# A written order for TensorE, ScalarE and VectorE in the expert stage of a two-layer decoder trunk

## The chip, the core and the metric

The kernel runs on one core of a Trainium2 chip. Its time is the device time of one execution in microseconds; lower is better. The core has separate instruction queues for TensorE (PE in the profile; its weight loads have a row of their own, PEld), VectorE (DVE), ScalarE (ACT), GpSimd (POOL) and SyncE (SP, which here only starts transfers). Each queue is worked off in the order in which its instructions stand, and an instruction whose input isn't ready holds everything behind it on the same queue.

## The reference, cut to what matters

The trunk has two layers. Each has a mixer (convolution heads beside attention heads) and a channel mixer; in layer 0 that is a dense SwiGLU, in layer 1 a mixture of eight experts of which every token takes two. There are 256 tokens of width 1024, and an expert is 3584 wide, all in float32:

```
def _swiglu(h, w_gate, w_up, w_down):
    return (jax.nn.silu(h @ w_gate) * (h @ w_up)) @ w_down

for e in range(N_EXPERTS):
    out = out + gates[:, e:e + 1] * _swiglu(t, w_gate[e], w_up[e], w_down[e])
```

The experts' weights are 8 x 3 x 3584 x 1024 float32 numbers, 352 MB, and each is read once.

## The kernel before, in words

Everything up to the routing (mixer, dense layer, mixer, router) takes the first 457 us and isn't touched. After it stands the **expert stage**, a straight-line program written by `expert_steps`.

**Tiles of weights.** A weight tile is about 0.9 MB: two 128-row pieces of `w_gate` or `w_up` (128x1792 numbers) or of `w_down` (128x2048, or 128x1024 for the last piece). SyncE loads it into one of seven `raw` buffers (L73). Then it is *converted* (`Gran.conv`): ScalarE writes a rounded copy `wh` (L192), VectorE writes the rest, `wl = raw - wh` (L193). TensorE multiplies with both. There are four `wh` and four `wl` buffers, so that a fifth tile's conversion waits until TensorE is done with the first.

**Products.** `products` (L883) issues the matmuls of a tile. An expert with more than 64 tokens takes three matmuls for each piece (wh, wl, and wh with the rest of the activations); one with at most 64 takes two, with the two parts of its tokens side by side in 128 columns, and later adds the lower half of the sums to the upper. The count is known only at run time, so `by_count` (L869) puts both versions into a branch on TensorE.

**Chunks.** An expert is cut into four chunks of 896 columns. A chunk has four gate tiles, four up tiles, and the four down tiles of the same chunk of the expert before it: twelve tiles in all. Their sums stand in PSUM banks `pg`, `pu` and `pd`, two each; two banks `pt` serve everything else.

**Late work.** When a sum is complete, other work follows on it:
- `low` (L967, ScalarE) copies the lower halves of a gate or up sum out of PSUM into `lo`, and `fold_` (L973, TensorE) adds them to the upper halves;
- `post` makes SiLU of the gate sum (L982, ScalarE) and multiplies with the up sum (L984, VectorE);
- `transposes` (L934, TensorE) turns that product, and `split` copies it out in two parts (L232 ScalarE, L233 VectorE), ready for the down tiles;
- `gather` picks the next expert's tokens; `rows_of` and `scatter` split a finished expert's rows, bring them back to token order and add them to `x` (L1040, VectorE).

**What sets the order.** `add` collects steps; a step with a tile has its `Gran`, whose conversion `drive` writes at most three tiles ahead, and `add_later` puts late work behind the next tile or the one after it. The order on each engine's queue isn't this list, though: a scheduler takes these steps in their order as priorities and moves instructions between the branches by its own estimate of when they are ready:

```
            while nxt < len(grans) and nxt < done + hl[1] and grans[nxt][1] not in held:
                grans[nxt][1].conv()
                nxt += 1
```

Of the kernel before, what the change touches and what calls it, by code (L numbers as in the profile page):

```python
# [14 lines left out]
P = 128  # L15
# [31 lines left out]
def trunk_kernel(ctx: ExitStack, tc, x_in, attn_norm, ffn_norm, w_in, b_in, conv_w, conv_b,  # L47
# [811 lines left out]
    def expert_steps(rnd):  # L859

        xg, ST, gt, gg, rxs = {}, {}, {}, {}, {}

# [20 lines left out]
        def gather(e):  # L885
            def run():
                m1, pt = moe["m1"], moe["pt"]
                Sm = m1.tile([P, NT, P], F32R, name="Sm")
                slots = slot1[:, rnd, :]
                if rnd == 0:  # L890

                    slots = m1.tile([P, P], F32, name="sl")
# [4 lines left out]
                x2 = xg[e] = m1.tile([P, KD, 2, P], F32R, name="xg", bufs=2)  # L897
                for q in range(2):
                    ps = pt.tile([P, 4, P], F32, name="pt")
                    for j in range(4):  # L900
                        d = slice((4 * q + j) * P, (4 * q + j + 1) * P)
                        for t in range(NT):
                            nc.tensor.matmul(ps[:, j, :], moe["hn"][:, t, d], f32(Sm[:, t, :]), start=(t == 0),
                                             stop=(t == NT - 1))
                    xq = x2[:, 4 * q:4 * q + 4]
                    split(xq[:, :, 0, :], xq[:, :, 1, :], ps)
                if e == 0 and rnd == 0:
                    moe["flags"]()
                    moe["weights"]()
                ps = pt.tile([P, 512], F32, name="pt")  # L910

                def rms(few):
                    for rows, cols in ((slice(P), slice(P)),) + ((slice(HP), slice(0, P, 2)),) * few:
                        for t in range(NT):
                            nc.tensor.matmul(ps[rows, 0:1], f32(Sm[:, t, cols]), moe["rs"][:, t:t + 1],
                                             start=(t == 0), stop=(t == NT - 1))
                by_count(e, rms)
                rxs[e] = m1.tile([P, 1], F32, name="rx", bufs=3)
                nc.scalar.copy(rxs[e], ps[:, :1])
                ps = pt.tile([P, NT, P], F32, name="pt")  # L920
                for t in range(NT):
                    nc.tensor.transpose(ps[:, t, :], f32(Sm[:, t, :]), ident)
                ST[e] = m1.tile([P, NT, P], F32R, name="ST", bufs=3)
                nc.scalar.activation(ST[e], ps, AF.Copy)
            return run

        def transposes(e, c):
            def run():
                g = gg[e, c]
                g2 = gt[e, c] = moe["m1"].tile([P, KJ, P, 2], F32R, name="g2", bufs=NCH)  # L930
                for j0, j1 in ((0, 4), (4, KJ)):
                    ps = moe["pt"].tile([P, 4, P], F32, name="pt")
                    for j in range(j0, j1):
                        nc.tensor.transpose(ps[:, j - j0, :], g[:, j * P:(j + 1) * P], ident)  # L934
                    split(g2[:, j0:j1, :, 0], g2[:, j0:j1, :, 1], ps[:, :j1 - j0, :])
            return run

        def proj(e, c, nm, w, pool):
# [4 lines left out]
            def step(k2):  # L943
# [14 lines left out]
                add(run, Gran((rnd, e, c, nm, k2), (2, CH), lambda t: [(t, wv[:, k2 * 2:k2 * 2 + 2, :])],  # L958
                              lambda t: t, DVE))
# [8 lines left out]

            def post():
                def fold_(few):  # L970
                    if few:
                        for hc in range(2):
                            nc.tensor.matmul(st["p"][hc][:HP, :HC], fold, moe["lo"][:, hc * HC:(hc + 1) * HC],  # L973
                                             start=False, stop=True)
                if rnd == 0:
                    by_count(e, fold_)
# [11 lines left out]
        yd = {}  # L988

        def down(e, c):  # L990
            wv = moe_w_down[0, e, c * CH:(c + 1) * CH, :].rearrange("(j p) c -> p j c", p=P)
            order = [(0, (0, 1)), (2, (0, 1)), (4, (0, 1)), (6, (0, 1))]
            if (e, c) == (NE - 1, NCH - 1):

                order[2:] = [(4, (0,)), (6, (0,)), (4, (1,)), (6, (1,))]

            def step(j0, chs):
                j1 = min(j0 + 2, KJ)

                def run(wh, wl):  # L1000
# [4 lines left out]
                    def mms(few):  # L1005
                        for j in range(j0, j1):
                            g_ = gt[e, c][:, j]
                            both = g_.rearrange("p s h -> p (s h)")[:, :P]
                            for i, ch in enumerate(chs):
                                o = slice(i * 512, (i + 1) * 512)  # L1010
                                products(yd[e, ch], (g_[:, :, 0], g_[:, :, 1], both), wh[:, j - j0, o], wl[:, j - j0, o],
                                         c == 0 and j == 0, c == NCH - 1 and j == KJ - 1, few)
                    by_count(e, mms)
                add(run, Gran((rnd, e, c, "d", j0), (j1 - j0, D), lambda t: [(t, wv[:, j0:j1, :])],
                              lambda t: t[:, :, chs[0] * 512:(chs[-1] + 1) * 512], DVE))
                if (e, c, chs) == (NE - 1, NCH - 1, (0,)) and j1 == KJ:
                    add_later(1, rows_of(e, (0,)))
                    add_later(2, scatter(e, (0,)))
            return [lambda a=a: step(*a) for a in order]

        ys = {}

        def rows_of(e, halves=(0, 1)):

            def run():
                for ch in halves:
                    y = ys[e, ch] = tmp.tile([P, 2, 512], F32R, name="h", bufs=3)
                    split(y[:, 0, :], y[:, 1, :], yd[e, ch])
            return run

        def scatter(e, halves=(0, 1)):
            def run():
                for ch in halves:
                    y = ys[e, ch]
                    for t in range(NT):
                        ps = moe["pt"].tile([P, 512], F32, name="pt")
                        for i in range(2):
                            nc.tensor.matmul(ps, ST[e][:, t, :], y[:, i, :], start=(i == 0), stop=(i == 1))  # L1038
                        xs = x[:, t, ch * 512:(ch + 1) * 512]
                        nc.vector.scalar_tensor_tensor(xs, ps, moe["gates"][:, t, e:e + 1], xs,  # L1040
                                                       op0=ALU.mult, op1=ALU.add)
            return run
# [3 lines left out]
        def do(fs, n=None):  # L1046
            for _ in range(len(fs) if n is None else min(n, len(fs))):
                fs.pop(0)()

        seq = [(e, c) for e in range(NE) for c in range(NCH)]  # L1050
        add(gather(0))
        for i, (e, c) in enumerate(seq):
            g = proj(e, c, "g", moe_w_gate, "pg")
            u = proj(e, c, "u", moe_w_up, "pu")
            d = down(e - 1, c) if e > 0 else []
# [8 lines left out]
            do(d, 1)  # L1064
            do(u, 1)
            if e > 1 and c == 0:
                add(scatter(e - 2))
            if c == 2 and e + 1 < NE:
                add(gather(e + 1))
            do(u, 1)  # L1070
            do(d, 1)
            do(u, 2)
            do(d)
        for c in range(NCH):
            d = down(NE - 1, c)
            if c == 0:
                add(rows_of(NE - 2))
            do(d, 3)
            if c == 0:
                add(transposes(*seq[-1]))  # L1080
                add(scatter(NE - 2))
            do(d)
        add(rows_of(NE - 1, (1,)))
        add(scatter(NE - 1, (1,)))
# [6 lines left out]
    n0 = len(steps)  # L1091
    expert_steps(0)
    held += [g for g, _ in steps[n0:] if g is not None][:AHEAD_E + 1]
    drive()

# [15 lines left out]
    with tc.If(big > P):  # L1111
        raw_t.clear()
        expert_steps(1)
        drive()
# [28 lines left out]
```

## Time and profile before

| | us |
|---|---|
| median of 3 runs | 1554.54 (1549.16 to 1554.97) |
| the profiled execution, its own time | 1559.1 |
| its span, first to last instruction | 1557.3 |
| outside the span | 1.8 |
| expert stage from the first product on | 457 to 1557.3 |

The profiled execution is 0.3% above the median. In the profile, the share of busy time of an engine is an average over stages; the expert stage is read by itself. Idle time "before" an instruction is put down to the engine whose result came last. A matmul's duration overlaps the next one's, so its start-to-start distance says what it costs in a row of them.

### The profile page before, as it was taken

How to read it: one execution, taken by the hardware profiler on the slowest of the kernel's cores; microseconds unless marked ns; L12 is line 12 of the kernel's file. 1: busy time of each engine (PE TensorE's matmuls, PEld its weight loads, DVE VectorE, ACT ScalarE, POOL GpSimd, SP SyncE). 2: the span in 40 equal slices, each digit the busy share in tenths (PEclk: the TensorE clock that was granted, in tenths of full speed). 3: DMA queues.
4: the chain of work that ended last, by engine and by line, in shares of the span. 5: the costliest groups of instructions: out<-in, count | busy, mean ns of one | idle time of the engine just before them, and what ended most of it. 6: DMA issues, size and time to landing. Idle time of an engine off the chain costs nothing. (4 is left out here: it accounts for less than half of the span.)

```text
span 1557.3 us, 19153 instructions
## 1 busy us (share of the span) xinstructions
PE 1381.4 (89%) x6963; PEld 1135.5 (73%) x6963; DVE 1172.4 (75%) x1155; ACT 1016.8 (65%) x1120; POOL 143.4 (9%) x99
## 2 busy tenths in 40 slices
PE   7989999989969888888889988998888889888986
PEld 6768999987656666677777876776777667676765
DVE  7776555577678887888778777877877787787776
ACT  5645444456458877777766676777677676667664
POOL 5531010065210000000000000000000000000000
PEclk9889999988989999999999999999999999999998
DMA  8634555642249999989888888989898988989882
GB/s 250 188 108 141 186 189 189 189 131 73 85 134 367 323 334 331 355 311 353 316 319 297 299 307 287 341 300 356 307 327 309 313 325 315 338 314 345 326 308 106
DMA packets 150179, 416.24 MB, mean 267 GB/s; under 512 B 8599, under 2 KB 49635, under 8 KB 150049
## 3 DMA queue, kind: packets, MB, share of 16 engines
q1 hardware_dynamic: 149760, 413.38, 75.8%
q8 instruction: 91, 1.49, 0.4%
q0 software_dynamic: 288, 1.05, 0.2%
q14 instruction: 40, 0.32, 0.1%
HBM read 413.35 MB, written 1.05 MB: 266 GB/s over the span
## 5 line engine op out<-in xcount | busy, mean ns | idle before, releaser
L193 DVE TENSOR_TENSOR wl<-raw,wh 128x1792 fp32r<-128x1792 f32 (+2 forms) x460 | 853.7, 1885 | 260.9 <-ACT wh L192 255.8
L192 ACT ACTIVATE wh<-raw 128x1792 fp32r<-128x1792 f32 (+2 forms) x496 | 753.6, 1553 | 173.7 <-PE cv L695 34.9
L883 PE MATMUL pg<-wh,xg 128*128 128x448 f32 x768 | 261.0, 383 | 10.6 <-PEq L869 5.3
L883 PE MATMUL pu<-wh,xg 128*128 128x448 f32 x768 | 253.9, 378 | 15.2 <-PEq L869 8.3
L883 PE MATMUL pd<-wh,g 128*128 128x512 f32 x672 | 246.4, 407 | 1.6 <-DVE h L233 1.6
L883 PE MATMUL pu<-wl,xg 128*128 128x448 f32 x512 | 197.0, 385 | 33.5 <-DVE wl L193 33.1
L883 PE MATMUL pg<-wl,xg 128*128 128x448 f32 x512 | 195.9, 383 | 34.6 <-DVE wl L193 34.5
L883 PE MATMUL pd<-wl,g 128*128 128x512 f32 x448 | 182.7, 408 | 12.5 <-DVE wl L193 12.5
L883 PEld LDWEIGHTS pu<-wh,xg 128*128 128x128 f32 x768 | 147.8, 192 | 41.2 <-issue 16.1
L883 PEld LDWEIGHTS pg<-wh,xg 128*128 128x128 f32 x768 | 149.8, 195 | 36.5 <-issue 12.0
L883 PEld LDWEIGHTS pd<-wh,g 128*128 128x128 f32 x672 | 131.8, 196 | 28.8 <-ACT lo L967 4.5
L883 PEld LDWEIGHTS pg<-wl,xg 128*128 128x128 f32 x512 | 100.3, 196 | 57.1 <-DVE wl L193 50.0
L883 PEld LDWEIGHTS pu<-wl,xg 128*128 128x128 f32 x512 | 100.1, 196 | 55.6 <-DVE wl L193 49.4
L883 PEld LDWEIGHTS pd<-wl,g 128*128 128x128 f32 x448 | 87.0, 194 | 40.3 <-DVE wl L193 25.7
L430 DVE SCALAR_TENSOR_TENSOR cv<-up,wcol,cv 128x256 f32<-128x256 f32 x226 | 98.3, 484 | 5.0 <-PE cv L404 3.0
L1099 POOL DMA_DIRECT2D h<-in_final_norm_dram x1 | 0.6, 599 | 1072.1 <-DVE x L1040 1072.1
L232 ACT ACTIVATE g<-pt 128x512 fp32r<-128x512 f32 x64 | 36.5, 575 | 82.9 <-PE pt L934 82.9
L193 POOL TENSOR_TENSOR wl<-raw,wh 128x1024 fp32r<-128x1024 f32 x36 | 86.1, 2406 | 38.6 <-ACT wh L192 38.3
L982 ACT ACTIVATE h<-pg,rx 128x448 f32<-128x448 f32 x64 | 40.0, 631 | 50.3 <-PEq L869 26.9
L353 PE MATMUL mm<-th,wh 128*128 128x256 f32 x224 | 65.8, 296 | 1.1 <-ACT sg L411 1.1
L967 ACT ACTIVATE lo<-pu 64x448 fp32r<-64x448 f32 x64 | 34.4, 541 | 48.7 <-PE pu L883 47.8
L353 PE MATMUL mm<-th,wl 128*128 128x256 f32 x224 | 65.3, 292 | 0.8 <-POOL wl L193 0.7
(236 smaller groups left out, 1818.2 us busy)
## 6 DMA issues: line engine op xcount, KB each, us to landing
raw<-in_moe_w_gate_dram SPq DMA_DIRECT2D x128, 896.0 KB
raw<-in_moe_w_up_dram SPq DMA_DIRECT2D x128, 896.0 KB
raw<-in_moe_w_down_dram SPq DMA_DIRECT2D x96, 1024.0 KB
raw<-in_moe_w_down_dram SPq DMA_DIRECT2D x32, 512.0 KB
raw<-in_ffn_w_gate_dram SPq DMA_DIRECT2D x11, 1024.0 KB
raw<-in_ffn_w_up_dram SPq DMA_DIRECT2D x11, 1024.0 KB
raw<-in_ffn_w_down_dram SPq DMA_DIRECT2D x11, 1024.0 KB
raw<-in_w_in_dram SPq DMA_DIRECT2D x10, 1024.0 KB
```

The lines of the kernel that those rows point to most:

```text
L192: nc.scalar.activation(self.h, src, AF.Copy)
L193: (lo or lo_eng()).tensor_sub(self.l, src, f32(self.h))
L232: nc.scalar.activation(hi, src, AF.Copy)
L353: nc.tensor.matmul(ps[:, :S], w(a, k), b[:, k, :], start=(n == 0), stop=(n == 3 * KD - 1))
L430: nc.vector.scalar_tensor_tensor(acc, up[:, c, k:k + S], w, acc, op0=ALU.mult, op1=ALU.add)
L883: nc.tensor.matmul(o, a, b, start=(first and i == 0), stop=(last and i == len(mm) - 1))
L967: nc.scalar.activation(moe["lo"][HP:, hc * HC:(hc + 1) * HC], st["p"][hc][HP:, :HC], AF.Copy)
L982: nc.scalar.activation(gg[e, c][:, o], ps, AF.Silu, scale=rxs[e])
L1099: nc.gpsimd.dma_start(fg, final_norm.unsqueeze(0).to_broadcast([P, D]))
```

## The change

The expert stage no longer goes through `add` and `drive`. `put` appends a tile to a list, and `at(mid, n, f)` or `at(end, n, f)` hang a piece of late work on tile n. `emit` then writes the tiles one after the other: first the conversions up to three tiles ahead, then the pieces hung on `mid`, then the products, then the pieces on `end`. All of it stands under `manual_schedule` for TensorE, ScalarE and VectorE: the queues of these three hold the instructions in the order in which they are written. SyncE's queue is not in that list. `gather`, `transposes` and `scatter` are cut into their TensorE part and their ScalarE and VectorE part, so that the two can stand on different tiles; `fold_` is cut off from `post`. The first expert's `gather` stands before the written part. The buffers, the tiles, the instructions' sizes and the loads stay; one transposed copy and one column share a `pt` bank that had one each.

```
+        def emit():
+            for n in range(max([len(order)] + [i + 1 for i in (*mid, *end)])):
+                for g, _ in order[n:n + AHEAD_E + 1]:
+                    g.conv()
+                for f in mid.get(n, ()):
+                    f()
+                if n < len(order):
+                    g, run = order[n]
+                    run(g.h, g.l)
+                for f in end.get(n, ()):
+                    f()
...
                 if k2 == KD // 2 - 1:
                     if rnd == 0:
-                        add_later(DEFER, low)
-                    add_later(DEFER + 1, post)
+                        at(mid, last() + 1, low)
+                        at(end, last() + 2, lambda: by_count(e, fold_))
+                    at(mid, last() + 3, post)
...
+                if c == NCH - 1 and j1 == KJ:
+                    n = last()
+                    if e < NE - 1:
+                        at(mid, n + 1, lambda: rows_of(e, both))
+                        for ch in both:
+                            at(end, n + 10 + 3 * ch, lambda ch=ch: scatter(e, ch))
+                            at(mid, n + 11 + 3 * ch, lambda ch=ch: residual_(e, ch))
...
-            do(g, 1)
-            if e > 1 and c == 0:
-                add(rows_of(e - 2))
-            do(g, 1)
-            do(d, 1)
-            do(g, 2)
-            if i > 0:
-                add(transposes(*seq[i - 1]))
...
+                n0 = len(order)
+                for fs, n in ((g, 2), (d, 1), (g, 2), (d, 1), (u, 2), (d, 1), (u, 2)):
+                    do(fs, n)
+                turn, parts = transposes(e, c)
+                at(end, last() + 6, turn)
+                at(mid, last() + 7, parts)
+                do(d, 1)
+                if c == 2 and e + 1 < NE:
+                    for (w, n), f in zip(((mid, 6), (end, 9), (mid, 10), (end, 12), (mid, 13)), gather(e + 1)):
+                        at(w, n0 + n, f)
...
+            with tc.manual_schedule(engines={E.PE, E.Activation, E.DVE}):
+                emit()
```

Two places show what moves. The first is ScalarE's queue where a product of the second expert has been transposed and is copied out (`g2`). Before; `wh` is a tile's conversion, `lo` the copy of lower halves:

```order
L967 ACTIVATE lo_4229<-pu_6234 64x448
L192 ACTIVATE wh_6389<-raw_6387 128x1792
L869 UNCONDITIONAL_BRANCH
L967 ACTIVATE lo_4229<-pu_6235 64x448
L869 UNCONDITIONAL_BRANCH
L192 ACTIVATE wh_6418<-raw_6416 128x2048
L869 UNCONDITIONAL_BRANCH
L232 ACTIVATE g2_6579<-pt_6580 128x512
L192 ACTIVATE wh_6437<-raw_6435 128x1792
L869 UNCONDITIONAL_BRANCH
L232 ACTIVATE g2_6579<-pt_6587 128x384
L192 ACTIVATE wh_6471<-raw_6469 128x1792
```

The same copy on ScalarE's queue in the changed kernel, where numbers of buffers differ:

```order
L192 ACTIVATE wh_6497<-raw_6495 128x2048
L895 UNCONDITIONAL_BRANCH
L192 ACTIVATE wh_6524<-raw_6522 128x1792
L895 UNCONDITIONAL_BRANCH
L192 ACTIVATE wh_6551<-raw_6549 128x1792
L895 UNCONDITIONAL_BRANCH
L192 ACTIVATE wh_6589<-raw_6587 128x2048
L232 ACTIVATE g2_6593<-pt_6578 128x512
L232 ACTIVATE g2_6593<-pt_6583 128x384
L1010 ACTIVATE lo_4229<-pg_6426 64x448
L1010 ACTIVATE lo_4229<-pg_6427 64x448
L192 ACTIVATE wh_6623<-raw_6621 128x1792
```

Before, the copy stood among conversions of the tiles that TensorE was about to multiply; now both halves stand together behind the conversion of `wh_6589`, and so do the two `lo` copies.

The second place is TensorE's queue at the transposes (`pt`) that these copies read. Before; they follow the products with `wh_6389`, and a tile of down products (`pd`) follows them:

```order
L883 MATMUL pg_6442<-wh_6389,xg_4955 128x448
L883 MATMUL pg_6442<-wl_6390,xg_4955 128x448
L869 UNCONDITIONAL_BRANCH
L934 MATMUL pt_6580<-ident_104,h_6260 128x128 x4
L934 MATMUL pt_6587<-ident_104,h_6260 128x128 x3
L869 COMPARE_AND_BRANCH
L883 MATMUL pd_5404<-wh_6418,g2_5483 128x512
L883 MATMUL pd_5404<-wl_6419,g2_5483 128x512
```

TensorE's queue at the same transposes in the changed kernel:

```order
L909 LDWEIGHTS zerob_144
L909 MATMUL pg_6427<-zerob_144 64x448
L895 UNCONDITIONAL_BRANCH
L971 MATMUL pt_6578<-ident_104,h_6271 128x128 x4
L971 MATMUL pt_6583<-ident_104,h_6271 128x128 x3
L895 COMPARE_AND_BRANCH
L909 MATMUL pd_5404<-wh_6497,g2_5527 128x512
```

The transposes moved from behind the chunk's second tile to behind its fifth (whose conversion is the one just ahead of `wh_6497`). Before, ScalarE's queue had one conversion, `wh_6418`, between the tile that TensorE multiplies ahead of the transposes and the copy that needs them; now it has four.

## Rows read from the trace of the kernel before

**Rows 1.** Windows by expert: us, busy PE, PEld, DVE, ACT, POOL (instructions), PEclk, DMA share, GB/s.

```profile
457.00:534.80 77.80, 69.02 (x332) 54.92 (x331) 65.33 (x48) 65.33 (x62) 0.00 (x0) 1.00 0.88 317
534.80:660.60 125.80, 109.51 (x469) 82.28 (x468) 106.07 (x71) 97.71 (x86) 0.00 (x0) 0.96 0.93 341
660.60:796.30 135.70, 120.86 (x571) 99.44 (x570) 109.66 (x76) 97.67 (x86) 0.00 (x0) 1.00 0.91 326
796.30:941.60 145.30, 132.49 (x626) 112.28 (x625) 110.28 (x76) 97.93 (x86) 0.00 (x0) 0.99 0.86 304
941.60:1081.10 139.50, 123.77 (x535) 97.61 (x534) 110.10 (x76) 97.90 (x86) 0.00 (x0) 0.95 0.88 319
1081.10:1219.50 138.40, 123.48 (x579) 101.81 (x578) 109.36 (x74) 97.65 (x86) 0.00 (x0) 0.99 0.90 317
1219.50:1356.50 137.00, 120.16 (x530) 95.10 (x529) 109.19 (x74) 97.90 (x86) 0.00 (x0) 0.98 0.89 324
1356.50:1492.70 136.20, 119.97 (x535) 98.16 (x535) 107.71 (x72) 96.40 (x82) 0.00 (x0) 0.97 0.90 325
```

**Rows 2.** The same view for the whole stretch of these eight windows.

```profile
457.00:1492.70 1035.70, 919.25 (x4164) 741.59 (x4163) 827.70 (x560) 748.48 (x660) 0.00 (x0) 0.98 0.89 321
```

**Rows 3.** Waits in 457 to 1492.7: who for whom, us, times, longest us.

```profile
DVE wl L193 <- ACT wh L192: 178.9, 135, 4.3
ACT g L232 <- PE pt L934: 78.2, 31, 3.8
PEld pg L883 <- DVE wl L193: 50.0, 44, 1.9
PEld pu L883 <- DVE wl L193: 49.4, 51, 1.9
...
PEld pd L883 <- DVE wl L193: 24.5, 39, 1.1
...
ACT wh L192 <- PE pd L883: 20.6, 28, 2.1
PEld L883 <- issue: 19.1, 64, 0.3
...
ACT rx L919 <- PE pt L915: 14.4, 6, 2.5
```

**Rows 4.** Timeline of ACT: start, us, what, times, idle time before it.

```profile
700.51 1.92 ACT L192 ACTIVATE wh<-raw 128x2048 fp32r<-128x2048 f32 x1
705.37 0.63 ACT L232 ACTIVATE g<-pt 128x512 fp32r<-128x512 f32 x1 [2.94 <-PE pt L934]
705.90 1.68 ACT L192 ACTIVATE wh<-raw 128x1792 fp32r<-128x1792 f32 x1
...
714.10 1.15 ACT L967 ACTIVATE lo<-pg 64x448 fp32r<-64x448 f32 x2 [1.14 <-PE pg L883]
```

**Rows 5.** Groups by form, 457 to 1492.7: busy us, mean ns, idle before.

```profile
L193 DVE TENSOR_TENSOR wl<-raw,wh 128x1792 fp32r<-128x1792 f32 x252 | 506.3, 2021 | 173.3 <-ACT wh L192 168.4 <-PE pg L883 4.8
...
L883 PEld LDWEIGHTS pg<-wh,xg 128*128 128x128 f32 x764 | 149.0, 195 | 36.5 <-issue 12.0 <-ACT wh L192 10.1 <-ACT h L982 1.2
...
L883 PEld LDWEIGHTS pd<-wh,g 128*128 128x128 f32 x558 | 109.8, 197 | 22.1 <-ACT lo L967 3.0 <-issue 0.6
```

**Rows 6.** Timeline of PE: products of one tile.

```profile
710.61 0.57 PE L883 MATMUL pg<-wh,xg 128*128 128x448 f32 x2
711.02 0.37 PE L883 MATMUL pg<-wl,xg 128*128 128x448 f32 x1
```

**Rows 7.** The chain that ended last, near its end: start, us, what.

```profile
1518.95 23.15 PE pd L883 x98
```

**Rows 8.** Waits of SyncE's queue in 457 to 1492.7.

```profile
SPq L73 <- DVE wl L193: 850.0, 357, 12.5
```

**Rows 9.** Windows of 10 us between 480 and 660, two of eighteen; columns as in rows 1.

```profile
570.00:580.00 10.00, 7.63 (x37) 5.66 (x35) 9.53 (x9) 8.23 (x7) 0.00 (x0) 1.00 1.02 409
...
590.00:600.00 10.00, 10.00 (x40) 7.99 (x39) 8.88 (x6) 7.71 (x7) 0.00 (x0) 0.86 0.99 327
```

More of the change, by code (lines that the diff above doesn't have):

```diff
@@ L863, in expert_steps, with at, put, last @@
         xg, ST, gt, gg, rxs = {}, {}, {}, {}, {}
+        order, mid, end = [], {}, {}
+        def at(where, n, f):
+            where.setdefault(n, []).append(f)
+        def put(run, gran):
+            order.append((gran, run))
+        def last():
+            return len(order) - 1
+        def emit():
[9 more added lines that the diff above has]
+                    f()
         def by_count(e, run):
@@ L914, in rms @@
                         for t in range(NT):
[L915 removed]
+                            nc.tensor.matmul(ps[rows, 3, 0:1], Sm[:, t, cols], moe["rs"][:, t:t + 1],
                                              start=(t == 0), stop=(t == NT - 1))
                 by_count(e, rms)
[L918 to L920 removed]
@@ L921, in run, with copies @@
                 for t in range(NT):
[L922 to L925, printed above, removed]
+                    nc.tensor.transpose(ps[:, t, :], Sm[:, t, :], ident)
+            def copies():
+                rxs[e] = m1([P, 1], F32, name="rx", bufs=3)
+                nc.scalar.copy(rxs[e], st["ps"][:, 3, :1])
+                ST[e] = m1([P, NT, P], F32R, name="ST", bufs=3)
+                nc.scalar.activation(ST[e], st["ps"][:, :NT, :], AF.Copy)
@@ L927, in transposes, with turn @@
+            return select, rows_, parts, turn, copies
         def transposes(e, c):
-            def run():
+            st = {}
+            def turn():
                 g = gg[e, c]
-                g2 = gt[e, c] = moe["m1"].tile([P, KJ, P, 2], F32R, name="g2", bufs=NCH)
[L931 to L935, printed above, removed]
@@ L957, in run @@
                     by_count(e, mms)
-                add(run, Gran((rnd, e, c, nm, k2), (2, CH), lambda t: [(t, wv[:, k2 * 2:k2 * 2 + 2, :])],
+                put(run, Gran((rnd, e, c, nm, k2), (2, CH), lambda t: [(t, wv[:, k2 * 2:k2 * 2 + 2, :])],
                               lambda t: t, DVE))
@@ L967, in low, with fold_ @@
                     nc.scalar.activation(moe["lo"][HP:, hc * HC:(hc + 1) * HC], st["p"][hc][HP:, :HC], AF.Copy)
-            def post():
[L970 to L976, printed above, removed]
+            def fold_(few):
+                if few:
+                    for hc in range(2):
+                        nc.tensor.matmul(st["p"][hc][:HP, :HC], fold, moe["lo"][:, hc * HC:(hc + 1) * HC],
+                                         start=False, stop=True)
+            def post():
                 if nm == "g":
@@ L1019, in down @@
[L1019 to L1042, printed above, removed]
@@ L1046, in do @@
-        def do(fs, n=None):
-            for _ in range(len(fs) if n is None else min(n, len(fs))):
-                fs.pop(0)()
[L1050 to L1055, printed above, removed]
-            do(g, 1)
-            if e > 1 and c == 0:
-                add(rows_of(e - 2))
-            do(g, 1)
-            do(d, 1)
-            do(g, 2)
-            if i > 0:
-                add(transposes(*seq[i - 1]))
[L1064 to L1073, printed above, removed]
+                if c == NCH - 1 and j1 == KJ:
[5 more added lines that the diff above has]
+                            at(mid, n + 11 + 3 * ch, lambda ch=ch: residual_(e, ch))
+                    else:
+                        at(mid, n + 1, lambda: rows_of(e, chs))
+                        at(end, n + 1, lambda: scatter(e, chs[0]))
+                        at(mid, n + 2, lambda: residual_(e, chs[0]))
@@ new lines, in down, with rows_of, scatter @@
+            return [lambda a=a: step(*a) for a in parts]
+        def rows_of(e, halves):
+            for ch in halves:
+                y = ys[e, ch] = tmp.tile([P, 2, 512], F32R, name="h", bufs=3)
+                split(y[:, 0, :], y[:, 1, :], yd[e, ch])
+        def scatter(e, ch):
+            for t in range(NT):
+                ps = pys[t] = moe["pt"].tile([P, 512], F32, name="pt")
+                for i in range(2):
+                    nc.tensor.matmul(ps, ST[e][:, t, :], ys[e, ch][:, i, :], start=(i == 0), stop=(i == 1))
@@ L1074, in expert_steps, with run @@
         for c in range(NCH):
             d = down(NE - 1, c)
[L1076 to L1084, printed above, removed]
+            do(d, len(d))
+        def run():
+            select, rows_, parts, turn, copies = gather(0)
+            select()
+            for q in range(2):
+                rows_((q,))
+            parts()
+            if rnd == 0:
+                moe["flags"]()
+                moe["weights"]()
+            turn()
+            copies()
+            E = mybir.EngineType
+            with tc.manual_schedule(engines={E.PE, E.Activation, E.DVE}):
+                emit()
@@ L1086, in trunk_kernel @@
+        return [g for g, _ in order], run
     mixer(0)
@@ L1090, in trunk_kernel @@
     add(lambda: urgent(route))
-    n0 = len(steps)
-    expert_steps(0)
-    held += [g for g, _ in steps[n0:] if g is not None][:AHEAD_E + 1]
+    grans, run_experts = expert_steps(0)
+    held += grans[:AHEAD_E + 1]
     drive()
+    run_experts()
     def finish():
```

71 lines of the change are left out of this document (46 added, 25 removed).

## The prediction

> **What bounds the kernel now.** I read the windows by expert first [rows 1]. From 457 us on each window is one expert: its gate and up tiles, and the down tiles of the expert before it (the first window has no down tiles). Full windows last 126 to 145 us, and in none is an engine full: VectorE is busy for 106 to 110 us, ScalarE for 96 to 98, the transfers run at a share of 0.86 to 0.93. Over the stretch of 1035.7 us VectorE works for 827.7 and ScalarE for 748.5 [rows 2]. Something makes them take turns.
>
> The waits say what [rows 3]. ScalarE waits for TensorE in eight groups of late work, from the transposed products (78.2) down to the gather's column (14.4), together 260.7 us, and 20.6 more for a free buffer. With its busy 748.5 that makes 1030 of the 1035.7: ScalarE is never idle for lack of a tile, it either works or is blocked at the head of its queue. The damage travels down the line: VectorE then waits 178.9 for `wh`, and TensorE's weight loads wait 50.0, 49.4 and 24.5, that is 124, for `wl`. The timeline shows one such case [rows 4]: at 702.4 ScalarE has converted a tile, then stands 2.94 us before the copy `g<-pt`, because TensorE is still in the products written ahead of the transposes, while the next conversion waits behind the copy. The transfers are not the cause: SyncE waits for `wl` to give a buffer back 357 times in this stretch [rows 8], so loads wait for conversions and not the other way.
>
> **The change, part by part.** No instruction is added or taken away in any amount that counts; what moves is when ScalarE and VectorE come to the late work.
>
> *ScalarE's waits.* In the written order every piece on `mid` of tile n stands behind the conversion of tile n+3, and that conversion reuses the buffers of tile n-1, so that it can't start before TensorE is done with n-1. A sum that ended with tile n-1 is thus complete when ScalarE reaches it. The transposes hung on `end` of a tile need some 0.9 us, and the conversion ahead of their copy takes 1.68 [rows 4]. So I put the 260.7 at nothing from below, and from above at what a buffer's way round allows (below).
>
> *What is late next.* I take for each window the largest of three needs.
>
> TensorE: matmuls overlap, so I count weight loads, which don't. A gate load takes 195 ns and a down load 197 [rows 5]; a gate product costs 0.205 us from start to start (0.41 for two) [rows 6] and a down product 0.236 (23.15 / 98) [rows 7]. With 2.74 gate or up loads to a down load (2 x 764 / 558) the factor is 1.09. To it I add 6 us a window for gaps named "issue" (19.1 and 12.0 are the shown ones [rows 3, 5], and up tiles have a group like the gate tiles'). From busy PEld [rows 1] this gives 66, 96, 114, 128, 112, 117, 110 and 113.
>
> VectorE: its busy time, 65, 106, 110, 110, 110, 109, 109 and 108.
>
> Transfers: a window's length times its GB/s is what it moved, 24.7 MB for the first, 42.9 for the second and about 44.3 for the rest. At which rate can they go? In 10 us windows from 480 to 660 eleven of eighteen have a share of 0.96 or more; they move 327 to 409 GB/s [rows 9], 373 in the mean. At 373 the needs are 66, 115, 119, 118, 119, 118, 119 and 119.
>
> The largest are 66, 115, 119, 128, 119, 118, 119 and 119, together 903: only the fourth window, where both experts have many tokens, is TensorE's. Against 1035.7 that would be a gain of 133.
>
> By busy matmuls instead of loads TensorE's need would be 69, 110, 121, 132, 124, 123, 120 and 120 and the sum 924. The Trainium skill (Perfetto Trace Analysis, Identifying the Most-Contended Engine) says that matmul busy time is no measure of headroom and that busy weight loads are; the rows agree (0.57 us "busy" for two products that start 0.205 apart), so I keep the loads.
>
> *What the buffers cost.* When TensorE ends a tile, its pair is refilled by 1.7 us on ScalarE and 2.02 on VectorE, 3.75 with the hand-offs. At the sixth tile of a chunk two copies of transposed products (1.15) and two `lo` (1.15 [rows 4]) stand between, and VectorE has 1.2 of its own: 7.3 in all. TensorE wants the pair three tiles later, at 903/368 = 2.45 a tile after 7.4. That fits where a tile has twelve products, but a tile of eight lasts 1.64, three of them 4.9, so that TensorE falls short by up to 2.4 a chunk in the sixteen chunks of the four experts with few tokens: 38 us at most. In these it isn't the bound, so the lower end is nothing; but VectorE and the transfers have nearly the same need, and what one of them loses isn't made up. I take the 38, 4% on 903, since three needs within a few per cent don't mesh without loss. The upper end is today's best window: 125.8 against its need of 115, 9%.
>
> *Smaller pieces.* A finished expert's two `pd` banks are read behind the fourth tile's conversion and wanted by the third tile's products: up to 3.4 us of TensorE seven times, 24 us, inside the 38 where TensorE has slack. The first expert's gather now stands whole ahead of the products, for 1 to 3 us in a window whose conversions were four tiles ahead; I count nothing. The tail after 1492.7 has TensorE in down products at 0.236 in either order; nothing. The stages before 457: unchanged.
>
> Sum: 903 x 1.04 = 939, a gain of 97. The profiled execution had 1559.1 (its span 1557.3 and 1.8 around it), so 1462 by it; it lies 4.6 above the median, so **1458** against 1554.54. With no loss it would be 1422, at 9% 1507.
>
> **Rivals.**
>
> *The transfers bind earlier.* In every window GB/s divided by share is 352 to 367 [rows 1], so that "full" may be no more than 360. Then six windows need 122 to 124 and the sum is 930; with the 4% 968, a gain of 68, 1487. If they never do better than today's best window, 341, it is 977 and about 1496 without any loss of meshing. For it: 327 at a share of 0.99. Against it: 409 at 1.02 [rows 9], and loads that start late today come in bursts. The Trainium skill (DMA: Bandwidth & Descriptors, Where 436 GB/s comes from) lets HBM's 358 GB/s a core bind here; an estimate by it is 44.3/0.358 = 124 a window, the same 1487; the row with 409 speaks against it for a core alone.
>
> *The waits come back as hand-offs*, VectorE for ScalarE and TensorE for VectorE at the heavy tiles, more than I allow: half the gain or less, 1507 to 1545.
>
> *Nothing changes:* ScalarE waits as long for free buffers as it did for sums, because TensorE sets the pace after all: 1555. Against it: 20.6 for buffers now, and 124 us in which TensorE itself waits for `wl`.
>
> *Slower:* the way of a pair becomes the bound. 368 tiles in 1035.7 are 2.81 each; four of them less a tile's own 2.05 leave 9.2 us for the way, which today is 3.75 at its shortest. From 9.2 on the written order loses. At 10.2 a tile would take 3.06, 92 us more: 1647. But the heaviest tile has 7.3, and seven of twelve carry nothing.
>
> **How the numbers follow.** The forecast (1425 to 1490, with the slower transfers' near end in it) gets 0.70, transfers that bind at 1490 to 1507 0.11, hand-offs 0.10, better than 1425 0.02, nothing 0.03, slower 0.04. 8 in 10 lie between **1428 and 1508**. A measurement of this kernel tells about 0.5% (7.8 us) from no change; faster by more than that is 0.93, the same 0.03, slower 0.04.
>
> **What would show it.** In the changed profile ScalarE's waits for TensorE's late work should fall from 260.7 to under 40, and its waits for a buffer should rise; TensorE's waits for `wl` should fall from 124 to under 70 and sit in the windows with few tokens; busy times of VectorE and ScalarE should stay at 828 and 748 in a stretch some 97 us shorter; DMA should stand at a share of 0.95 or more and some 355 GB/s. The fourth window should still be the longest, near 133. I'm wrong in the step on ScalarE if waits for `pt`, `pu` or `pg` remain; in the rate of the transfers if ScalarE begins to wait for `raw`; in the 4% if all waits are short and VectorE is still under 85% busy.

## The result and the profile after

The changed kernel takes **1449.39 us** (median of 4 runs, 1448.06 to 1456.52) against 1554.76 of the kernel before on the same chip: a ratio of 0.9339, 95% interval 0.9302 to 0.9376. The forecast was 1458, range 1428 to 1508, faster with 0.93.

The profiled execution took 1448.06 with a span of 1446.3. Of the 111 us to the profiled execution of before, 10.2 lie ahead of the expert stage, whose first product starts at 443.7 instead of 453.9 (the 457 given for it ahead of the prediction is the second tile's start). The instructions of TensorE, VectorE and ScalarE stand in the same order in both up to the first expert's gather, where 10.1 of the 10.2 are already there (437.89 against 448.02), and in the fourteen profiles of this study the start lies anywhere from 441.9 to 453.9. So I compare the **stage**, from the first gate product to the end of the span: 1103.4 before, 1002.6 after.

The windows by expert of the changed kernel, cut at the same tiles as in [rows 1] (the first from the first product on, the last one the tail; columns as there), and the stretch of the first eight:

```profile
443.70:521.50 77.80, 71.02 (x341) 58.83 (x339) 63.69 (x45) 63.18 (x60) 0.00 (x0) 0.96 0.87 321
521.50:634.40 112.90, 104.34 (x481) 81.72 (x481) 105.81 (x72) 99.88 (x91) 0.00 (x0) 1.00 0.99 374
634.40:755.40 121.00, 115.20 (x564) 99.09 (x563) 108.90 (x77) 97.78 (x86) 0.00 (x0) 1.00 0.97 369
755.40:891.20 135.80, 129.35 (x630) 112.51 (x629) 109.93 (x75) 100.12 (x86) 0.00 (x0) 1.00 0.90 332
891.20:1013.30 122.10, 115.62 (x536) 95.68 (x535) 108.79 (x76) 98.50 (x87) 0.00 (x0) 0.99 0.95 353
1013.30:1136.30 123.00, 116.89 (x574) 100.56 (x573) 109.14 (x76) 98.98 (x86) 0.00 (x0) 1.00 0.96 363
1136.30:1257.90 121.60, 115.13 (x534) 95.20 (x533) 108.74 (x76) 98.47 (x87) 0.00 (x0) 0.99 0.95 360
1257.90:1376.30 118.40, 112.49 (x533) 96.14 (x532) 107.17 (x70) 97.42 (x82) 0.00 (x0) 1.00 0.98 375
1376.30:1446.30 70.00, 51.03 (x210) 40.67 (x208) 45.32 (x38) 33.32 (x37) 2.00 (x3) 0.88 0.46 175
...
443.70:1376.30 932.60, 880.05 (x4181) 739.74 (x4180) 822.17 (x560) 754.32 (x661) 0.00 (x0) 0.99 0.95 357
```

The seven full windows went from 957.9 to 854.8 us, each by 9.5 to 17.8. TensorE is busy for 809.0 of them, before for 850.2 [rows 1], so that it stands idle for 46 us instead of 108. VectorE and ScalarE work as long as before [rows 2]; DMA went from 0.89 to 0.95.

The waits in this stretch, as in [rows 3]:

```profile
DVE wl L193 <- ACT wh L192: 105.6, 108, 4.4
ACT wh L192 <- PE pd L909: 86.4, 53, 3.5
ACT wh L192 <- PE pg L909: 45.6, 42, 4.6
ACT wh L192 <- PE pu L909: 23.8, 29, 2.6
...
PE pd L909 <- ACT wh L192: 13.0, 6, 3.3
ACT xg L232 <- PE pt L934: 12.0, 8, 4.1
...
PEld pu L909 <- DVE wl L193: 7.4, 11, 1.5
```

Of ScalarE's eight groups of waits for late work one is left, `xg`, with 12.0 us of the 260.7. In their place ScalarE waits 155.8 for a free buffer (`wh` for `pd`, `pg`, `pu`), from 20.6. TensorE's loads wait 10.4 for `wl` (7.4 here, 2.5 and 0.5 at the other sums), from 124. New is a wait of TensorE's down products for ScalarE, six times, once for each change of expert.

### The profile page after: what moved, and what is told of

Its sections match the earlier page's. It is cut to its first block, busy times and chain, and to the rows that moved or that the text cites. A ratio compares the mean times of both kernels' runs of the same rounds, so it can differ in the third digit from the quotient of the medians.

```text
span 1446.3 us, 19143 instructions
## 1 busy us (share of the span) xinstructions
PE 1331.2 (92%) x6963; PEld 1126.8 (78%) x6963; DVE 1166.7 (81%) x1155; ACT 1022.5 (71%) x1120; POOL 143.6 (10%) x99
## 5 line engine op out<-in xcount | busy, mean ns | idle before, releaser
L909 PE MATMUL pg<-wh,xg 128*128 128x448 f32 x768 | 253.4, 374 | 7.9 <-ACT lo L1010 3.4
L909 PE MATMUL pu<-wl,xg 128*128 128x448 f32 x512 | 190.8, 373 | 3.9 <-DVE wl L193 3.8
L909 PE MATMUL pg<-wl,xg 128*128 128x448 f32 x512 | 188.0, 367 | 0.0
L909 PE MATMUL pd<-wl,g 128*128 128x512 f32 x448 | 179.1, 400 | 0.8 <-DVE wl L193 0.7
L909 PEld LDWEIGHTS pg<-wh,xg 128*128 128x128 f32 x768 | 146.5, 191 | 29.8 <-ACT lo L1010 8.6
L353 PE MATMUL mm<-tl,wh 128*128 128x256 f32 x224 | 63.0, 282 | 0.6 <-DVE tl L290 0.6
L720 PE MATMUL acc<-wh,pp 128*128 128x512 f32 x176 | 50.3, 397 | 0.0
L695 PE MATMUL cv<-tl,wh 128*128 128x256 f32 x176 | 49.2, 280 | 0.3 <-DVE tl L290 0.3
```

The source lines that it names most:

```text
L353: nc.tensor.matmul(ps[:, :S], w(a, k), b[:, k, :], start=(n == 0), stop=(n == 3 * KD - 1))
L695: nc.tensor.matmul(ps, a[:, k, :], b[:, k, :], start=(n_ == 0), stop=(n_ == 3 * KD - 1))
L720: nc.tensor.matmul(st["o"][t][cc], a[:, kk, tk], b[:, 0, cc * 512:(cc + 1) * 512], start=(first and i == 0), stop=(last and i == 2))
L909: nc.tensor.matmul(o, a, b, start=(first and i == 0), stop=(last and i == len(mm) - 1))
```

## Experiments

All against the kernel before on the same chip. "Stage" is the stage of the profiled execution; the changed kernel itself is the second row. e5, e6 and e9 leave work out and compute something else, so their times only tell what that work costs.

| kernel | median us | ratio, 95% interval | stage us |
|---|---|---|---|
| before | 1554.76 | 1 | 1103.4 |
| changed | 1449.39 | 0.9339 (0.9302 to 0.9376) | 1002.6 |
| e1_list_only | 1555.28 | 1.0019 (0.9992 to 1.0045) | 1104.4 |
| e2_scalar_only | 1441.91 | 0.9297 (0.9260 to 0.9334) | 993.5 |
| e3_tensor_vector_only | 1605.88 | 1.0334 (1.0294 to 1.0373) | 1157.6 |
| e4_ahead_two | 1427.36 | 0.9210 (0.9154 to 0.9267) | 980.1 |
| e5_no_loads | 1452.17 | 0.9351 (0.9326 to 0.9377) | 1002.4 |
| e6_half_wl | 1428.73 | 0.9195 (0.9165 to 0.9226) | 984.6 |
| e7_down_late | 1439.98 | 0.9263 (0.9224 to 0.9302) | 987.9 |
| e8_fold_later | 1465.25 | 0.9425 (0.9395 to 0.9454) | 1013.9 |
| e9_half_products | 1346.62 | 0.8677 (0.8655 to 0.8700) | 897.8 |
| e10_three_pairs | 1511.67 | 0.9747 (0.9723 to 0.9771) | 1066.3 |
| e11_two_copies_later | 1434.96 | 0.9258 (0.9228 to 0.9288) | 982.0 |
| e12_two_scalar_only | 1433.79 | 0.9244 (0.9229 to 0.9260) | 985.5 |

### Which engine's order counts: e1, e2, e3

The theory is the prediction's: ScalarE's queue was blocked at its head. The rivals are that the new list with its smaller pieces brings the gain, or TensorE's order of the products.

```
-            with tc.manual_schedule(engines={E.PE, E.Activation, E.DVE}):
-                emit()
+            emit()                                                      e1
+            with tc.manual_schedule(engines={E.Activation}):            e2
+            with tc.manual_schedule(engines={E.PE, E.DVE}):             e3
```

> The rewritten list of the expert stage stays (late work handed to a later tile, smaller pieces of products, conversions two tiles further ahead in the list), but no engine is made to keep that list's order: the scheduler decides the rows, as it did before the change. In the order it makes, ScalarE's cast of a tile's part g2 stands one conversion behind the tile that is multiplied, as in the kernel before. Theory (ScalarE's queue, blocked at its head by late work, was the loss): the waits of ScalarE for transposes and sums come back, 100 us or more of them, and the time is 1530 to 1560. Rival (the rewritten list with its smaller pieces brings the gain, whoever orders it): 1445 to 1460.

> The written order is kept by ScalarE alone; TensorE's and VectorE's rows are the scheduler's. Theory (ScalarE's order is what counts): 1450 to 1475, ScalarE's waits for transposes and sums below 40 us. Rival (the order of the products on TensorE, or VectorE's, is what counts): above 1500.

> The opposite half: TensorE and VectorE keep the written order, ScalarE's rows are the scheduler's. Theory (ScalarE's order is what counts): above 1500, with ScalarE waiting for transposes and sums for 100 us or more. Rival (TensorE's and VectorE's order): 1450 to 1475.

The list alone gives nothing (1.0019), and in its profile ScalarE waits for eight groups of late work as before, 265.9 us in the first eight windows against 260.7 [rows 3]. In e3 such waits stand beside waits for buffers. The three largest in e1:

```profile
ACT g L232 <- PE pt L971: 64.0, 31, 3.4
...
ACT lo L1010 <- PE pu L909: 44.0, 22, 2.7
...
ACT h L1024 <- PEq L895: 35.9, 16, 4.9
```

and in e3:

```profile
ACT g L232 <- PE pt L971: 104.1, 30, 6.2
ACT wh L192 <- PE pg L909: 52.9, 21, 7.3
ACT wh L192 <- PE pd L909: 50.6, 48, 2.7
```

ScalarE's order alone (e2) gives the whole gain, and its profile has 4.1 us of waits for `xg` and 2.6 for `h` as the only late work above 1 us. This is the theory, with two surprises of size. e2 came out 8 us below its range. And e3 isn't merely without gain: TensorE and VectorE that keep the written order, against a ScalarE that doesn't, lose 54 us of the stage. e2's lines:

```profile
ACT xg L232 <- PE pt L934: 4.1, 1, 4.1
ACT h L1024 <- PEq L895: 2.6, 5, 0.8
```

Whether the order on TensorE and VectorE is worth anything beside ScalarE's isn't settled: e2 has 9 us less in the stage than the changed kernel, but the intervals of the two times overlap.

### What binds the stage now: e5, e6, e9

The prediction had the transfers as the largest need in six of seven full windows. e5 takes them away, e6 halves VectorE's work on a tile of two pieces, and e9 takes away a third of TensorE's matmuls (one product of two, or of three).

```
e5  -            t = raws.tile([P] + list(shape), F32, name="raw")    (and its load)
    +            raw_t[key] = seven[n % RAWS]
e6  -                (lo or lo_eng()).tensor_sub(self.l, src, f32(self.h))
    +                nc.vector.tensor_sub(self.l[:, :1], src[:, :1], f32(self.h)[:, :1])
e9  -            mm = [(ps, b, wh), (ps, b, wl)] if few else [(ps, h, wh), (ps, h, wl), (ps, l, wh)]
    +            mm = [(ps, b, wl)] if few else [(ps, h, wl), (ps, l, wh)]
```

> Leaves out the transfers of the expert stage: seven tiles of one w_down are loaded once, and every tile is converted from these seven (so the products are of other weights than the reference's). Nothing else changes. Theory (transfers bind the windows with few tokens, TensorE and VectorE the others): the second to the eighth window fall together by 10 to 40 us, most of it in those at 0.95 or more of DMA time, with the second at about 106 us by VectorE: 1410 to 1440. Rival (TensorE, the meshing of three engines over four buffer pairs, binds everywhere): within 6 us of the changed kernel, 1443 to 1456.

> Leaves out half of each wl: VectorE subtracts for one of a tile's two halves, and TensorE multiplies by that half twice. VectorE's share of a tile falls by about half. Theory (VectorE's and TensorE's turns mesh imperfectly, transfers are next): VectorE's waits for wh rise, buffers come free no earlier, and the total falls by 0 to 20 us, 1430 to 1450. Rival (VectorE's 2 us for a tile still paces the windows of about 110 us): a fall of 30 us or more, below 1420.

> Leaves out the products with wh in the experts' sums: TensorE multiplies by wl alone, one product in place of two (two in place of three where an expert has many tokens); every conversion, transfer and hand-off stays. First theory (TensorE's own products bind the stage now, 880 us of 933; after them the transfers do at the 374 GB/s of the second window): the seven full windows and the first, 933 us together, fall to about 890 at a DMA share of 0.98 or more, the tail loses 20 to 30 us, and the total is 1370 to 1400. Second theory (transfers are faster when asked for more, and VectorE's 822 us come next): about 850 for the windows and 1330 to 1365 in all. Rival (the waits between the engines over four pairs of buffers bind, not TensorE's work): above 1425.

My theory for e5 fell, and with it the prediction's largest term; the rival's 1443 to 1456 holds. The second and fourth window of e5:

```profile
522.80:635.80 113.00, 104.25 (x481) 81.78 (x481) 105.85 (x72) 99.96 (x91) 0.00 (x0) 1.00 0.01 1
...
756.90:892.80 135.90, 129.35 (x630) 112.51 (x629) 109.93 (x75) 100.06 (x86) 0.00 (x0) 1.00 0.00 1
```

The DMA share went from 0.99 to 0.01, and the window from 112.9 to 113.0. None of the nine stretches changed by more than 0.4 us. A full share only says that seven loads are always on their way: in the changed kernel SyncE still waits for a buffer for 758.0 of the 929.3 us from 447 on, and ScalarE waits for `raw` once, 0.7 us.

```profile
SPq L73 <- DVE wl L193: 758.0, 358, 12.5
```

e9 shows the other half, and its second theory (1330 to 1365) holds. With 2775 matmuls in place of 4181 the windows fall until VectorE is full. The second and fourth, and the stretch of eight:

```profile
520.00:629.10 109.10, 84.43 (x289) 55.32 (x287) 105.44 (x72) 98.92 (x89) 0.00 (x0) 0.81 1.02 399
...
739.40:851.30 111.90, 97.00 (x450) 78.56 (x449) 108.16 (x76) 98.92 (x87) 0.00 (x0) 0.98 1.02 395
...
451.00:1289.00 838.00, 675.94 (x2775) 499.47 (x2774) 814.86 (x561) 746.41 (x662) 0.00 (x0) 0.91 1.01 396
```

VectorE is busy for 814.9 of 838.0 us and the transfers move 396 GB/s, so 373 was no ceiling. Nor are the transfers the bound there at a share of 1.01: SyncE still waits 663.7 us for buffers, and ScalarE 14.1 for `raw`. All seven full windows are alike, 107.7 to 111.9, where the changed kernel's differ with the experts' tokens: in that kernel it is TensorE, its own products and its pauses, that sets them. e6 lies between its two cases, just under the first: 842.0 for the seven windows against 854.8, and 72.5 for the first against 77.8. Half of VectorE's work on the tiles is thus worth 18 us of the stage, and part of that is a shorter wait at `pd` (7.3 us in place of 13.0).

### The banks of a finished expert: e7

The six waits at `pd` are the prediction's "smaller piece": four of 1.60 to 1.74 us and two of 3.16 and 3.28. TensorE, ScalarE and VectorE in the changed kernel where the fourth expert's sums are read (start, us, what, times, idle time before it):

```profile
899.75 0.36 PE L909 MATMUL pg<-wl,xg 128*128 128x448 f32 x1
903.28 0.55 PE L909 MATMUL pd<-wh,g 128*128 128x512 f32 x1 [3.16 <-ACT wh L192]
903.62 0.63 PE L909 MATMUL pd<-wl,g 128*128 128x512 f32 x1
904.05 1.05 PE L909 MATMUL pd<-wh,g 128*128 128x512 f32 x2
```

```profile
895.82 1.92 ACT L192 ACTIVATE wh<-raw 128x2048 fp32r<-128x2048 f32 x1 [2.15 <-PE pd L909]
897.76 0.97 ACT L1010 ACTIVATE lo<-pu 64x448 fp32r<-64x448 f32 x2
898.76 1.71 ACT L192 ACTIVATE wh<-raw 128x1792 fp32r<-128x1792 f32 x1
900.49 1.08 ACT L232 ACTIVATE h<-pd 128x512 fp32r<-128x512 f32 x2
```

```profile
900.50 2.03 DVE L193 TENSOR_TENSOR wl<-raw,wh 128x1792 fp32r<-128x1792 f32 x1 [0.44 <-ACT wh L192]
902.45 1.28 DVE L233 TENSOR_TENSOR h<-pd,h 128x512 fp32r<-128x512 f32 x2
```

The releaser named, `wh`, was done long before; what TensorE waits for is VectorE's reading of the banks, which follows ScalarE's at 900.49 and a `wl` of its own; and ScalarE's stands behind a conversion that waited 2.15 us for its buffer, `lo`, and one more conversion. After the pause the down products start 0.43 us apart in place of 0.233, at a granted clock of 0.54, the lower of the two levels (1.2 of 2.4 GHz); before it and a few us later it is 1.00. Behind the wait of 3.28 (from 1147.80 on) the clock is 0.72 over 3.5 us; behind the four shorter ones it stays at 1.00.

```profile
895.00:899.90 4.90, 4.08 (x20) 3.37 (x18) 2.86 (x2) 4.03 (x4) 0.00 (x0) 1.00 1.01 377
903.30:906.60 3.30, 3.30 (x8) 2.57 (x9) 3.30 (x4) 1.67 (x1) 0.00 (x0) 0.54 1.02 365
907.70:910.60 2.90, 2.90 (x15) 2.55 (x13) 1.35 (x1) 1.08 (x1) 0.00 (x0) 1.00 0.47 129
```

e7 puts the expert's first down tile behind four gate tiles.

```
-                for fs, n in ((g, 2), (d, 1), (g, 2), (d, 1), (u, 2), (d, 1), (u, 2)):
+                for fs, n in ((g, 4), (d, 1), (u, 1), (d, 1), (u, 1), (d, 1), (u, 2)):      (c == 0)
```

> Moves one thing in the written order: the first down tile of an expert comes after four gate tiles, not after two, so that the banks pd have been read out when its products start. Theory (the wait for these banks, with the lower granted clock behind it, costs each expert some 3 to 6 us): ScalarE's and TensorE's waits at pd, 13 to 15 us in sum, go, and the total falls by 8 to 25 us to 1425 to 1441. Rival (what is waited for there is made good by the conversions that go on meanwhile): within 6 us, 1443 to 1456.

As the theory had it: the group is gone from the waits, the seven windows are 840.4 in place of 854.8 and the stage is 14.7 shorter. The tail is as long as before (69.7): it has no gate tiles to put ahead.

### How far ahead the conversions stand: e4, e10

```
e4   -                for g, _ in order[n:n + AHEAD_E + 1]:
     +                for g, _ in order[n:n + AHEAD_E]:
e10  -AHEAD_E = 3
     +AHEAD_E = 2                (this also makes one wh and one wl buffer less)
```

> Everything of the change but one number: the conversions stand two tiles ahead of the products in the written order, not three, so that one conversion fewer lies between a sum's end and the work of ScalarE on it, with the same four pairs of buffers. Theory (a queue is blocked where late work stands too near): ScalarE's waits for late work stay below 60 us, since the work is still a tile late, but TensorE waits again for wl, and the time rises by 25 to 70 us to 1475 to 1520. Rival (where the conversions stand doesn't matter so long as the late work is late): within 10 us of the changed kernel, 1440 to 1460.

> The conversions two tiles ahead, as in e4_ahead_two, but with three pairs of buffers in place of four, so that a conversion again needs the pair of the tile multiplied just before. Theory (two tiles ahead was faster since a conversion that waits for its pair blocks ScalarE's queue, and with four pairs one tile of slack lies there): ScalarE's waits for pairs go from 67 back to 130 us or more, and the time to 1440 to 1465. Rival (it was faster since late work had one conversion fewer ahead of it): within 8 us of e4_ahead_two, 1420 to 1435.

Both readings given for e4 fell: of the kernels that leave no work out it is the fastest, 22 us ahead of the changed kernel. TensorE does wait longer for `wl`, 35.4 us (below, and 5.7 at `pu`) from 10.4, and ScalarE waits for late work again. But ScalarE's waits for buffers fell from 155.8 to 67.4, and TensorE's pause at `pd` is as good as gone. Waits in e4:

```profile
ACT g L232 <- PE pt L971: 44.1, 30, 3.1
ACT wh L192 <- PE pd L909: 31.3, 56, 1.7
ACT xg L232 <- PE pt L934: 26.5, 15, 4.1
PEld pg L909 <- DVE wl L193: 22.7, 27, 1.9
ACT wh L192 <- PE pg L909: 22.5, 30, 1.7
...
ACT wh L192 <- PE pu L909: 13.6, 19, 1.1
...
PEld pd L909 <- DVE wl L193: 7.0, 11, 0.9
```

With conversions three ahead and four pairs, a conversion wants the pair of the tile that TensorE has just multiplied. It is then itself the instruction that blocks the head of ScalarE's queue, and late work that is ready (the reading of `pd`) stands behind it. The same place in e4 (ScalarE, then TensorE):

```profile
887.58 1.09 ACT L232 ACTIVATE h<-pd 128x512 fp32r<-128x512 f32 x2
...
890.63 0.48 PE L909 MATMUL pd<-wh,g 128*128 128x512 f32 x1 [0.65 <-DVE h L233]
```

The seven windows of e4 are 839.8, as short as e7's 840.4; another 5.4 us come from the first window (72.4 for 77.8) and 2.1 from the tail.

e10 asked whether the slack in the pairs does this or the smaller number of conversions ahead of late work. Its waits:

```profile
ACT wh L192 <- PE pd L909: 113.8, 64, 3.5
ACT wh L192 <- PE pg L909: 62.6, 55, 2.7
PEld pg L909 <- DVE wl L193: 51.2, 66, 2.1
ACT wh L192 <- PE pu L909: 39.0, 38, 2.6
PEld pd L909 <- DVE wl L193: 36.3, 33, 1.9
```

Waits for buffers are back at 215.4 as the theory says, but the time is 84 us above e4's, far beyond both readings: with one pair less TensorE also runs out of tiles (96.1 us of loads waiting for `wl`, 8.6 of them at `pu`). It speaks for slack and against the rival, but it changes two things at once, so the share of each is open; no run has five pairs, which would show slack alone.

### Two pieces that gave nothing: e8, e11, and the best two together: e12

```
e8   -                        at(end, last() + 2, lambda: by_count(e, fold_))
     +                        at(end, last() + 3, lambda: by_count(e, fold_))
     -                    at(mid, last() + 3, post)
     +                    at(mid, last() + 4, post)
e11  e4, and
     -                at(mid, last() + 7, parts)
     +                at(mid, last() + 8, parts)
```

(e11 also moves two of the gather's pieces by one tile; e12 is e4 with ScalarE's order alone.)

> The work on ended sums is put one more tile late (the casts and transposes behind a gate or up sum). Theory (TensorE still waits some 18 us for lo and g of such work): these waits go and the total falls by 3 to 12 us, 1437 to 1447. Rival (the transfers or the buffers take up what is saved, or banks come free later and products wait for them): no change or up to 10 us slower, 1447 to 1460.

> The conversions two tiles ahead with four pairs, and ScalarE's casts of transposes and of gathered rows one tile later than in e4_ahead_two. There ScalarE waited 71 us for these transposes. If such waits still cost time, they fall below 25 us and the total by 3 to 12 us to 1415 to 1424. Rival (TensorE is the bound and ScalarE's waits lie beside its products): 1422 to 1433.

> The two best so far together: the conversions two tiles ahead in the written order, and that order kept by ScalarE alone, with TensorE's and VectorE's rows left to the scheduler. If ScalarE's order is all that counts and TensorE's products are the bound, the time is that of e4_ahead_two or a little less, 1412 to 1428. Rival (with less slack in the buffers the scheduler's rows make TensorE wait for ScalarE's late work): 1432 to 1455.

e8 missed on the other side of both readings: 16 us slower. TensorE's waits for `lo` went but for 3.5 us, but its down products wait 24.0 us at fifteen places (named `wh` again) in place of 13.0 at six, and 13.3 more for its own sequencer (`PEq`). Work that is one tile later also hands its results on later; which of the two moved pieces does this isn't separated. e11 took most of ScalarE's waits for transposes away (4.0 us are left of 44.1 and 26.5, while `lo` waits 45.8) and gained nothing, at 2 us above the rival's range. That such waits lie beside TensorE's products, as the rival has it, fits this and isn't shown by itself. e12 ends at e4's time within the intervals, 16 us below the changed kernel; by its median it lies 6 us above the theory's range and 2 inside the rival's, so that it doesn't decide between them.

What ScalarE waits for buffers isn't the price by itself. It is 157.2 us in e2, 155.8 in the changed kernel, 126.9 in e12 and 67.4 in e4, and e12 with nearly twice e4's has nearly its time. What goes with the time is how long TensorE stands idle in the seven windows: 108 us before, 46 in the changed kernel, 40 in e2, 38 in e12, 36 in e4, 35 in e7. In e2, e4, e7 and e12 no wait at `pd` reaches 1.5 us.

## Why the prediction was right, step by step

**ScalarE's waits**, from 260.7 to below 40: right, 12.0, and e1 to e3 show that this step carries the gain. Only "from below nothing" was too kind to the order: it made conversions block the same queue. e7, which takes away the waits at `pd`, and e4, which also gives the buffers slack, put the price at 15 to 22 us of the stage.

**The largest of three needs**: the sum came out, its terms didn't. The seven full windows were to take 837 x 1.04 = 870 and took 854.8. *Transfers*, 115 to 119 a window: wrong, they bind nothing (e5) and run at 396 GB/s when asked (e9). The step that failed is "at which rate can they go": I took what transfers did in busy moments, while their buffers came back late [rows 8, 9], for what they can do. *TensorE* by loads, 790 for the seven: about right. If each start-to-start distance between its matmuls is put at the usual one of its kind (205 ns for gate and up, 232 for down, 111 for transposes, 300 beside the fold's one-row product) wherever it is longer, the records of the seven windows add up to some 770 in the changed kernel and before alike; my 790 has 42 of gaps in it. *VectorE*: right, 109 a window, and full in e9.

**The 4% for meshing** was therefore too small, and that the sum came out is luck in part. Without transfers the largest needs of the seven are 106, 114, 128, 112, 117, 110 and 113, in all 800: the transfers put 37 too much into the sum, and of the 55 by which 854.8 lies above 800 the 4% had 33. What the 4% was taken from was wrong too: TensorE short of a refilled pair in the windows with few tokens, 38 us at most. Its loads wait 10.4 for `wl` in the whole stretch. e6 and e7 take 12.8 and 14.4 of the 55; as both shorten the wait at `pd`, the two can't be added. Of the rest the waits show, over all eight windows, 13.7 us of TensorE for `lo` and 11.9 for its own sequencer (`PEq`), in pauses of at most 1.1 us; what each is worth wasn't measured.

**Busy loads or busy matmuls.** By busy matmuls I would have had 850 for the seven windows, nearly the time itself, but for a poor reason: the busy of a matmul grows with pauses and at the lower clock (a down product: 0.48 us behind the pause that ends at 1147.83, 0.63 at the lower clock at 904.90, 0.39 otherwise), so that the stretch has 922 us of it before and 880 after, for the same products. The Trainium skill (Perfetto Trace Analysis, Identifying the Most-Contended Engine) was right that loads show the need, which the 770 bears out. The same section of the Trainium skill says that occupancy misleads for DMA, because there are sixteen engines. e5 agrees that it misled, with a share of 0.99 that could be removed for nothing; whether the sixteen engines are the reason no run here shows.

**Smaller pieces.** The `pd` banks: up to 3.4 us seven times was right in place, and in size for the six in the full windows (1.60 to 3.28, 13.0 in all, with slow products behind the two longest; 14.4 by e7); the seventh, in the tail, is 6.2. But "inside the 38" counted it where TensorE has slack, and e7 shows that it has none there. The first window was to shrink to 66 x 1.04 = 69, from 77.8 that left out its first tile; from the first product on it went from 80.9 to 77.8 only. The tail was to stay and grew from 64.7 to 70.0: once more the reading of `pd` comes late, TensorE stands 6.2 us, and its products then start at the lower clock:

```profile
1379.76 0.40 PE L909 MATMUL pd<-wl,g 128*128 128x512 f32 x1
1386.32 0.77 PE L909 MATMUL pd<-wh,g 128*128 128x512 f32 x1 [6.16 <-DVE h L233]
```

**The rivals.** Transfers at 360 (1487) are refuted by e9's 396 GB/s; in the Trainium skill (DMA: Bandwidth & Descriptors, Where 436 GB/s comes from) the 358 GB/s would have been the ceiling, and the measurement decides against it for this lone core. Hand-offs that eat half the gain (1507 to 1545) and no change (1555) fell by the time itself, although ScalarE's waits for buffers did rise to 155.8. A pair's way round as the bound wasn't reached with four pairs; e10 shows how near it is, with three. The marks named were met: `wl` waits 10.4 (8.8 of them in the second window, the full one with the fewest matmuls), busy 822 and 754, DMA 0.95 and 357 GB/s, the fourth window the longest with 135.8. But "DMA at 0.95" was no sign of what I took it for.

## What to carry to other kernels

Where queues are strictly in order, look for the engine whose busy time and waits together fill the span, and ask of each wait what stands behind it: only that engine's order was worth writing here, and writing that of its partners alone made things worse. Work that waits for an old sum and work that waits for a free buffer block the queue alike, so that a prefetch as deep as its buffers left no slack here. A full DMA share was no bound here, and the sign was the queue that starts loads, which spent its time waiting for buffers; take the loads out, or halve the suspected engine's work, before putting a rate into a sum.

## What I had not expected of the hardware

- A pause of 3.16 us on TensorE, in a stretch granted the full clock, was followed by 3.3 us at 0.54; the four of 1.60 to 1.74 in the same profile and one of 0.65 in e4 by full clock. The length of one pause doesn't tell alone: in e2 one of 1.70 us, ending at 892.09, and one of 1.18, ending at 894.01, go with 0.50 from 893.3 to 899.5. From 903.28 to 907.70 stand twelve products, 4.42 us in place of 2.8 at 0.233, so that the pause cost half as much again as it lasted.
- All loads of the stage gone or all present: the granted clock and the durations stayed (fourth window of e5 against that of the changed kernel, 109.93 and 109.93 us of VectorE). Transfers at 332 GB/s took nothing measurable from VectorE and ScalarE there.
- The first part of the program, which the change leaves alone, ended anywhere between 441.9 and 453.9 us. In the profile before, the granted clock of its pieces at 50 to 100 and 350 to 400 was 0.86, in the one after 0.97; so some 10 us between two single profiles need not come from a change.
